# Turning the first two x1 chunks into token columns by DMA transposes of 16-bit planes

## The chip, the cores and the metric

The kernel runs on one core of a Trainium2 chip. The core has TensorE (matrix products, PE in the profile; its weight loads are PEld), VectorE (DVE), ScalarE (ACT), GpSimd (POOL) and SyncE (SP, which here only issues DMAs). Each engine works through its own queue in the order in which the program was written, and semaphores make one engine wait for another. The metric is device microseconds of one execution; lower is better.

## The reference

One encoder layer on x of 512 tokens by 2048 columns, all in float32:

```
h = RMSNorm(x);  q, k, v of A and B = h @ W_in
A = grouped-query attention, axial rotary;  B = dilated windowed attention, partial rotary
x1 = x + concat(RMSNorm(A), RMSNorm(B)) @ W_out
out = RMSNorm(x1 + SwiGLU(RMSNorm(x1)))
```

The change lies between the third line and the fourth. W_out makes x1 with tokens on the partitions (four tiles of 128 tokens), in four chunks of 512 columns. The gate and up products of SwiGLU need x1 the other way round: its columns on the partitions and the 512 tokens along the row, as the operand that TensorE holds. So each 128 x 128 block of x1 has to be transposed, 64 blocks in all.

## The kernel before, in words

**Products.** A float32 operand is split into a high part rounded to the format that TensorE takes fast (ScalarE, a Copy) and the low rest (VectorE, a subtraction). `mm3` (L226) makes three products: high by high (L228), high by low (L229), low by high (L230). The low part of a weight is thus needed at the second matmul. In the gate/up and down products a scheme of seven products of sums (forms) takes the place of eight.

**Units.** The program is a list of units, written out by the loop at L1552 to L1571. In W_out a unit is 128 rows of weights by 512 columns: four token tiles by three matmuls, 12 in all. Mixer A's four chunks come first, then mixer B's four chunks of eight units each, and then the gate/up blocks. Ahead of the matmuls of unit n, `prepare(n)` (L1515) writes: loads of weights up to LOAD_AHEAD = 24.0 planned us ahead at UNIT_US = 2.6 a unit, which is nine units (`Raw.load`, L273, on SP, two units per load); the high part of a weight up to SPLIT_AHEAD = 10.0 ahead, which is unit n+3 (L301, ScalarE); and the low part one unit behind that, unit n+2 (L306, VectorE).

**Side tasks.** Small work is kept in a list `side`. After each unit `give(1.0)` (L725) hands out tasks worth 1.0; a task costs 1.0 unless `weighed` (L674) gives it another cost. So the place of a task in the queues is behind the matmuls of one unit and ahead of `prepare` of the next.

**Around the change.** When mixer B's chunk c is summed up, `post` (L1120) adds it into x1 on VectorE (L1125, four rows), squares it on ScalarE (L1077), and puts tasks into `side`: two empty ones for c = 0 and one for the other chunks (`wait`, L1131), then for each of the chunk's two pairs of column blocks three tasks `h_side(i, half)` (L1165), and at the end `park_x1` (L1152), four DMAs on SP that store x1 in DRAM, where later stages add to it. The last chunk has an order of its own. In `h_side`, halves 0 and 1 transpose four blocks each on TensorE into a PSUM bank (L1171), and ScalarE moves them out with the gain as scale into the tile `pair` (L1174). After half 1 `pair_sums` makes four sums of pieces on VectorE (L379, in `form_sums`). Part 2 splits the pair into high and low parts in the tile `arena`: two casts on ScalarE (L1182), two subtractions on VectorE (L1184).

**A part that the change repeats.** The gate/up blocks already transpose their results by DMA: `planes` (L1255) copies the 32-bit words of a tile into a plane of their 16-bit halves, `turn` (L1258) transposes it by one DMA from SP, and `merge` (L1264) puts the halves together again, all copies on ScalarE.

Of the kernel before, what the change touches and what calls it, by code (L numbers as in the profile page):

```python
# [11 lines left out]
F32 = mybir.dt.float32  # L12
BF16 = mybir.dt.bfloat16
F32R = mybir.dt.float32r
U16 = mybir.dt.uint16
AF = mybir.ActivationFunctionType
# [4 lines left out]
P = 128  # L21
# [3 lines left out]
NT = S // P  # L25
# [41 lines left out]
COLUMN_BLOCKS = 3  # L67
SUM_LEAD = 6
ATTEND_PAST = 4


def f32(ap):
# [4 lines left out]
def encoder_block(ctx, tc, x, w_in, g_q_a, g_k_a, w_out, w_gate_up, w_down, g_final, x_t, gains, c_ident, c_mask,  # L77
                  c_axial, c_partial, out):
    nc = tc.nc
# [3 lines left out]
    sp = ctx.enter_context(tc.tile_pool(name="slots"))  # L83
# [5 lines left out]
    def nm(base):  # L89
        counter[0] += 1  # L90
        return f"{base}_{counter[0]}"

    def slot(base, dtype=F32, shape=(P, 512)):
        return sp.tile(list(shape), dtype, tag="s", name=nm(base))
# [57 lines left out]
    ident, gm, gf, go = fixed[:, :P], fixed[:, P:P + 16], fixed[:, P + 16:P + 32], fixed[:, P + 32:P + 48]  # L152
# [85 lines left out]
    class Pair:  # L238
        def __init__(self):
            self.parts = [sp.tile([P, 512], F32R, tag="tw", bufs=2 * TWINS, name=nm("tw")) for _ in range(2)]  # L240
# [72 lines left out]
    side = deque()  # L313
# [5 lines left out]
    def wait(n):  # L319
        side.extend([lambda: None] * n)  # L320
# [56 lines left out]
    def form_sums(a_l, a_r, b_l, b_r, s1, s2, s3, s4):  # L377
        def tt(out, x, y, op=OP.subtract):
            nc.vector.tensor_tensor(out, x, y, op=op)  # L379
        tt(s1, a_r, b_r, OP.add)  # L380
        tt(s3, a_l, a_r)
        tt(s2, s1, a_l)
        tt(s4, b_l, s2)
# [148 lines left out]
    def rope_partial(q):  # L532
        rot = q.rearrange("p t (h d) -> p t h d", h=4)[:, :, :, :PARTIAL]
        tmp = turning.rearrange("p (t h c) -> p t h c", t=NT, h=4)
        hp = PARTIAL // 2
        for s in range(2):
            nc.vector.tensor_tensor(
                tmp[:, :, :, s * hp:(s + 1) * hp], rot[:, :, :, (1 - s) * hp:(2 - s) * hp],
                ropeb[:, 1, :, s * hp:(s + 1) * hp][:, :, None, :].to_broadcast([P, NT, 4, hp]), op=OP.mult)
        nc.vector.tensor_tensor(rot, rot, ropeb[:, 0][:, :, None, :].to_broadcast([P, NT, 4, PARTIAL]), op=OP.mult)  # L540
        nc.vector.tensor_tensor(rot, rot, tmp, op=OP.add)

    oT = {}
    o_dram = {(g, h): dp.tile([P, 512], F32, tag=f"o{g}{h}", name=f"o{g}{h}")
# [129 lines left out]
    def weighed(cost, f):  # L674
        f.cost = cost
        return f
# [167 lines left out]
    class Half(Unit):  # L844
# [27 lines left out]
        def part(self, j):  # L872
            lo = self.i % 2 * 512
            return (self.duo.hi, self.duo.lo)[j][:, lo:lo + 512]
# [197 lines left out]
    x1 = {}  # L1072
# [6 lines left out]
    def out_chunk(kind, c):  # L1079
        box = {}  # L1080
        base = 0 if kind == "A" else NHA
        order = [6, 7, 0, 1, 2, 3, 4, 5] if (kind, c) == ("B", NC - 1) else list(range(NHA))

        def early(k):
            if (kind, k) not in oS and k >= SPILLED[kind]:
                drain_until(lambda: (kind, k) in oT)
                oS[kind, k] = split(oT.pop((kind, k)), "oS", go[:, base + k:base + k + 1],
                                    at=O_HOMES[kind][2 * k:2 * k + 2] if kind == "A" or k < 7 else None)

        class Back:  # L1090
            def __init__(self, k):
                self.k = k

            def load(self):
                drain_until(lambda: (kind, self.k) in oT)
                self.t = slot("oback")
                nc.sync.dma_start(self.t, o_dram[kind, self.k])

            def split_hi(self):
                hi, lo = oS[kind, self.k] = [place(*h) for h in O_HOMES[kind][2 * self.k:2 * self.k + 2]]  # L1100
                nc.scalar.activation(hi, self.t, AF.Copy, scale=go[:, base + self.k:base + self.k + 1])

            def split_lo(self):
                hi, lo = oS[kind, self.k]
                nc.vector.scalar_tensor_tensor(lo, self.t, go[:, base + self.k:base + self.k + 1], f32(hi),
                                               op0=OP.mult, op1=OP.subtract)

        def mm(u, n):
            k = order[n]
            if n == 0:  # L1110
                box["ps"] = [bank() for _ in range(NT)]
                if kind == "A":
                    whole = slot("x1", F32, (P, NT, 512))
                    x1[c] = [whole[:, t] for t in range(NT)]
                    for t in range(NT):
                        nc.sync.dma_start(x1[c][t], x[0, t * P:(t + 1) * P, c * 512:(c + 1) * 512])
            by_rows(u, n, NHA, lambda i, w, t: mm3(box["ps"][t], cols(oS[kind, order[i]], t * P), w, i == 0,
                                                   i == NHA - 1), post, kind == "A")

        def post(rows):  # L1120
            drain_until(lambda: kind in ro)
            if (kind, c) == ("B", 0) and 0 in rows:
                nc.scalar.activation(slot("table")[:, :1], ones, AF.Silu)
            for t in rows:
                nc.vector.scalar_tensor_tensor(x1[c][t], box["ps"][t], ro[kind][:, t:t + 1], x1[c][t],  # L1125
                                               op0=OP.mult, op1=OP.add)
                release(box["ps"][t])
                if kind == "B" and c < NC - 1:
                    square_x1(c, t)
            if kind == "B" and NT - 1 in rows:  # L1130
                wait(2 if c == 0 else 1)  # L1131
                if c == NC - 1:
                    side.extend(lambda p=p: h_side(2 * c, p, True) for p in range(4))
                    side.append(lambda: [square_x1(c, t) for t in (0, 1)])
                    side.extend(lambda p=p: h_side(2 * c + 1, p, True) for p in range(2))
                    side.append(lambda: park_x1(c))
                    side.append(lambda: [square_x1(c, t) for t in (2, 3)])
                    side.extend(lambda p=p: h_side(2 * c + 1, p, True) for p in range(2, 4))
                    side.append(make_r2)
                    return  # L1140
                for i in (2 * c, 2 * c + 1):
                    for part in range(3):
                        side.append(lambda i=i, part=part: h_side(i, part))
                side.append(weighed(0.0, lambda: park_x1(c)))
        add_chunk(w_out, [(base + k) * P for k in order], [(c * 512, 0, 512)], mm, None,
                  early if kind == "B" or c == 0 else None,
                  (lambda k: [Back(k)] if k < SPILLED[kind] else []) if c == 0 else None, tag="wa" if kind == "A" else "wo")
# [4 lines left out]
    def park_x1(c):  # L1152
        for t in range(NT):
            nc.sync.dma_start(x1_dram[c, t], x1[c][t])

    def pair_sums(w):
        def part(n):
            return w[:, n * 256:(n + 1) * 256]
        a_r, a_l, s3, s2, b_l, b_r, s1, s4 = (part(n) for n in range(8))
        form_sums(a_l, a_r, b_l, b_r, s1, s2, s3, s4)  # L1160

    hf = [False] * (KD // 2)
    hpart = {}

    def h_side(i, half, apart=False):  # L1165
        if half < 2:
            k = 2 * i + half
            c, j = divmod(k, 4)
            ps = bank()
            for n, t in enumerate((2, 3, 0, 1) if half == 0 else range(NT)):  # L1170
                nc.tensor.transpose(ps[:, n * P:(n + 1) * P], x1[c][t][:, j * P:(j + 1) * P], ident)  # L1171
            if half == 0 and not hpart:
                hpart[0] = sp.tile([P, 4 * 512], F32, tag="pair", bufs=1, name=nm("pair"))
            nc.scalar.activation(hpart[0][:, half * 1024:half * 1024 + 512], ps, AF.Copy, scale=gf[:, k:k + 1])  # L1174
            release(ps)
        if half == 1:
            pair_sums(hpart[0])
        if half >= 2:
            src = hpart[0][:, 256:].rearrange("p (f c) -> p f c", c=256)
            for t, part in ((arena[0], src[:, :EARLY]), (arena[1], src[:, EARLY:])):  # L1180
                if half == 2:
                    nc.scalar.activation(t[:, :, i, 0], part, AF.Copy)  # L1182
                if half == 3 or not apart:
                    nc.vector.tensor_tensor(t[:, :, i, 1], part, f32(t[:, :, i, 0]), op=OP.subtract)  # L1184
        if half == (3 if apart else 2):
            hf[i] = True
# [294 lines left out]
    at = [0.0]  # L1481
# [61 lines left out]
    pair = in_turn(twins, TWINS, [P, 2, 512], F32R, "tw")  # L1543
# [85 lines left out]
```

## Time and profile before

| | us |
|---|---|
| median of 3 runs | 1952.29 |
| lowest and highest run | 1951.33, 1952.58 |
| the profiled execution | 1951.23 |
| its span, first to last instruction | 1949.4 |
| granted TensorE clock (1 is full) | 0.999 |
| first and last transpose of x1 on TensorE (L1171) start | 613.8, 691.9 |

A row of the timeline reads: start, duration, engine, line, operation, tile written <- tiles read, shapes, count; in brackets the idle time before it and who ended it. A row of a group gives the least, median and greatest duration in ns and the first and last start. A row of waits gives the waiting engine and line, whom it waited for, the sum in us, how many times, and the longest. For a DMA the timeline has the time that its issue holds the queue; its landing is counted from the start of the issue. All times are microseconds from the start of the span unless marked ns.

### The profile page before, as it was taken

To read this page: it belongs to the slowest core of one execution; us is meant where nothing else is said; L and a number is where in the kernel's file an instruction comes from. 1 tells how busy PE (TensorE), PEld (TensorE's weight loads), DVE (VectorE), ACT (ScalarE), POOL (GpSimd) and SP (SyncE) were. 2 spreads that over 40 slices of the span, in tenths; PEclk is the share of its full clock that TensorE was granted. 3 is DMA by queue.
4 is the path that set the end of the run, shared out by engine and by line. 5 is a ranking of instruction groups with operands and counts; after the bars stand their busy time and mean duration, and the time that the engine had idled before them with its cause. 6 is when DMAs were issued, how large, how long until landed. Compare 5 with 4: busy or idle time off the path is not lost.

```text
span 1949.4 us, 24583 instructions
## 1 busy us (share of the span) xinstructions
PE 1937.3 (99%) x8743; PEld 1599.7 (82%) x8743; DVE 1536.5 (79%) x2012; ACT 1123.3 (58%) x1643; POOL 140.1 (7%) x184
## 2 busy tenths in 40 slices
PE   9999999999999999999999999999999999999998
PEld 7888888888888888888888888888888888888886
DVE  7987768888775697778778777787788978787887
ACT  7755554565455565555555555565555666565555
POOL 1000011000000000000000000000000121111121
PEclk9999999999999999999999999999999999999999
DMA  9677693144342557758767768678587799868865
GB/s 347 233 263 231 212 284 111 59 152 146 103 147 97 184 182 218 268 149 283 233 185 273 224 204 286 183 243 292 141 285 268 212 242 272 229 162 245 235 144 172
DMA packets 252028, 409.30 MB, mean 210 GB/s; under 512 B 58688, under 2 KB 85824, under 8 KB 251776
## 3 DMA queue, kind: packets, MB, share of 16 engines
q1 hardware_dynamic: 221072, 321.12, 50.6%
q0 software_dynamic: 22480, 60.57, 12.4%
q10 hardware_dynamic: 8352, 26.05, 4.1%
q8 instruction: 68, 1.11, 0.2%
q14 instruction: 56, 0.46, 0.1%
HBM read 334.52 MB, written 62.65 MB: 204 GB/s over the span
## 4 chain that ended last, share of the span: by engine, by line
PE 96%; DVE 3%; issue 1%; ACT 0%; DMA 0%; DVEq 0%; POOLq 0%; POOL 0%; SPq 0%; ACTq 0%
PE b L228 31%; PE b L230 31%; PE b L229 31%; PE b L613 1%; PE b L1171 0%; PE b L563 0%; DVE x L1125 0%; DVE w L306 0%; DVE ra L460 0%; DVE tw L896 0%; DVE qA L463 0%; PE b L790 0%; DMA stage<-in_w_in_dram 0%; PE b L574 0%; DVE qA L469 0%
## 5 line engine op out<-in xcount | busy, mean ns | idle before, releaser
L837 ACT ACTIVATE wide<-raw 128x1024 fp32r<-128x1024 f32 x462 | 487.1, 1058 | 455.3 <-PE b L230 265.4
L228 PE MATMUL b<-wide,arena 128*128 128x512 f32 x1848 | 719.6, 389 | 0.0
L840 DVE TENSOR_TENSOR wide<-raw,wide 128x1024 fp32r<-128x1024 f32 x462 | 561.7, 1221 | 200.4 <-ACT wide L837 192.8
L229 PE MATMUL b<-wide,arena 128*128 128x512 f32 x1848 | 719.0, 389 | 0.0
L230 PE MATMUL b<-wide,arena 128*128 128x512 f32 x1848 | 719.0, 389 | 0.0
L229 PEld LDWEIGHTS b<-wide,arena 128*128 128x128 f32 x1848 | 347.0, 188 | 72.1 <-DVE wide L840 0.3
L230 PEld LDWEIGHTS b<-wide,arena 128*128 128x128 f32 x1848 | 347.0, 188 | 71.9
L228 PEld LDWEIGHTS b<-wide,arena 128*128 128x128 f32 x1848 | 347.0, 188 | 71.6
L973 DVE TENSOR_TENSOR raw<-raw,raw 128x1024 f32<-128x1024 f32 x264 | 320.8, 1217 | 10.1 <-DMA raw<-in_w_gate_up_dram 10.1
L229 PE MATMUL b<-tw,arena 128*128 128x512 f32 x396 | 154.3, 390 | 0.6 <-DVE tw L896 0.6
L230 PE MATMUL b<-tw,arena 128*128 128x512 f32 x396 | 154.3, 390 | 0.0
L228 PE MATMUL b<-tw,arena 128*128 128x512 f32 x396 | 154.1, 389 | 0.0
L893 ACT ACTIVATE tw<-stage 128x512 fp32r<-128x512 f32 x140 | 85.4, 628 | 69.4 <-DVE stage L973 43.9
L896 DVE TENSOR_TENSOR tw<-stage,tw 128x512 fp32r<-128x512 f32 x140 | 93.5, 685 | 22.0 <-ACT tw L893 21.9
L228 PE MATMUL b<-w,arena 128*128 128x512 f32 x240 | 95.8, 399 | 0.0
L219 ACT ACTIVATE pTh<-b 128x512 fp32r<-128x512 f32 x64 | 38.2, 597 | 99.8 <-PE b L613 98.1
L230 PE MATMUL b<-w,arena 128*128 128x512 f32 x240 | 93.9, 391 | 0.0
L229 PE MATMUL b<-w,arena 128*128 128x512 f32 x240 | 93.5, 390 | 0.0
L229 PEld LDWEIGHTS b<-tw,arena 128*128 128x128 f32 x396 | 74.3, 188 | 16.7 <-DVE tw L896 1.4
L230 PEld LDWEIGHTS b<-tw,arena 128*128 128x128 f32 x396 | 74.3, 188 | 16.0 <-DVE arena L347 0.3
L228 PEld LDWEIGHTS b<-tw,arena 128*128 128x128 f32 x396 | 74.3, 188 | 15.4
L379 DVE TENSOR_TENSOR pair<-pair 128x256 f32<-128x256 f32 x120 | 46.4, 421 | 46.8 <-ACT pair L1174 23.2
(234 smaller groups left out, 2096.1 us busy)
## 6 DMA issues: line engine op xcount, KB each, us to landing
raw<-in_w_gate_up_dram SPq DMA_DIRECT2D x308, 512.0 KB, 6.3
raw<-in_w_down_dram SPq DMA_DIRECT2D x88, 512.0 KB, 7.7
stage<-in_w_in_dram SPq DMA_DIRECT2D x111, 256.0 KB, 5.3
forms<-pair POOLq DMA_DIRECT2D x22, 896.0 KB, 6.5
fr<-forms ACTq DMA_DIRECT2D x35, 512.0 KB, 6.2
raw<-in_w_out_dram SPq DMA_DIRECT2D x32, 512.0 KB, 4.1
x1d<-s POOLq DMA_DIRECT2D x54, 256.0 KB, 6.8
stage<-in_w_in_dram SPq DMA_DIRECT2D x90, 128.0 KB, 3.5
```

Source lines behind the costliest of these rows:

```text
L219: nc.scalar.activation(hi, src, AF.Copy)
L228: nc.tensor.matmul(dst, ah, bh, start=start, stop=False, skip_group_check=chained)
L229: nc.tensor.matmul(dst, ah, bl, start=False, stop=False, skip_group_check=chained)
L230: nc.tensor.matmul(dst, al, bh, start=False, stop=stop, skip_group_check=chained)
L379: nc.vector.tensor_tensor(out, x, y, op=op)
L613: nc.tensor.transpose(ps[:, t * P:(t + 1) * P], self.p[t][:, kb * P:(kb + 1) * P], ident)
L837: nc.scalar.activation(self.hi, self.src, AF.Copy)
L840: nc.vector.tensor_tensor(self.lo, self.src, f32(self.hi), op=OP.subtract)
L893: nc.scalar.activation(self.pair[:, 0], self.src, AF.Copy)
L896: nc.vector.tensor_tensor(self.pair[:, 1], self.src, f32(self.pair[:, 0]), op=OP.subtract)
L973: nc.vector.tensor_tensor(t[dst], t[src[0]], t[src[1]], op=OP.add if form == "m6" else OP.subtract)
```

## The change

For chunks 0 and 1 of x1 the transposes go by DMA. A class `Turned` holds the steps: `part(t)` copies token tile t (128 x 512 words) into a plane of 1024 16-bit halves on ScalarE, `turn(t)` transposes that plane by one DMA from SP into `words`, and `merge(h)` puts the halves of one column block together on ScalarE. `turned_x1(c)` gives the list of tasks that takes the place of the six `h_side` tasks and the parking at the end: pieces 0 and 1; transposes 0 and 1 with pieces 2 and 3; transposes 2 and 3, then parking; halves 0 and 1; the first pair's split and half 2; half 3 and the second pair's split. Tasks joined by a comma cost 0.5 each. A half is now a merge (two copies for an even one, one for an odd one) and the scaling by the gain. One empty task stands ahead of chunk 0's, not two. Chunks 2 and 3 are transposed on TensorE as before.

```diff
+X1_BY_DMA = 2
+    class Turned:
+        def __init__(self, whole):
+            self.whole, self.planes, self.words = whole, {}, None
+
+        def part(self, t):
+            p = self.planes[t] = slot("plane", U16, (P, 1024))
+            src = self.whole()[:, t].bitcast(U16).rearrange("p (h c s) -> p h s c", h=4, s=2)
+            nc.scalar.activation(p.rearrange("p (h s c) -> p h s c", h=4, s=2), src, AF.Copy)
+
+        def turn(self, t):
+            if self.words is None:
+                self.words = slot("words", U16, (P, NT, 8, P))
+            nc.sync.dma_start_transpose(self.words[:, t], self.planes.pop(t))
+
+        def merge(self, h, runs=((0, NT),)):
+            m, at = slot("merged"), 0
+            for lo, hi in runs:
+                src = self.words[:, lo:hi, 2 * h:2 * h + 2].rearrange("p t s c -> p t c s")
+                dst = m[:, at:at + (hi - lo) * P].bitcast(U16)
+                nc.scalar.activation(dst.rearrange("p (t c s) -> p t c s", c=P, s=2), src, AF.Copy)
+                at += (hi - lo) * P
+            return m
...
+                    x1["whole", c] = whole
...
-                wait(2 if c == 0 else 1)
+                wait(2 if c == 0 and not X1_BY_DMA else 1)
...
+                if c < X1_BY_DMA:
+                    side.extend(turned_x1(c))
+                    return
...
+    def turned_x1(c):
+        turned, i = Turned(lambda: x1["whole", c]), 2 * c
...
+        def half(j):
+            k = 4 * c + j
+            if not hpart:
+                hpart[0] = sp.tile([P, 4 * 512], F32, tag="pair", bufs=1, name=nm("pair"))
+            m = turned.merge(j, ((0, NT),) if j % 2 else ((2, NT), (0, 2)))
+            at = j % 2 * 1024
+            nc.scalar.activation(hpart[0][:, at:at + 512], m, AF.Copy, scale=gf[:, k:k + 1])
+            if j % 2:
+                pair_sums(hpart[0])
+        return [lambda: parts(0, 1), lambda: [turns(0, 1), parts(2, 3)],
+                weighed(0.5, lambda: turns(2, 3)), weighed(0.5, lambda: park_x1(c)), weighed(0.5, lambda: half(0)), weighed(0.5, lambda: half(1)),
+                weighed(0.5, lambda: h_side(i, 2)), weighed(0.5, lambda: half(2)), weighed(0.5, lambda: half(3)),
+                weighed(0.5, lambda: h_side(i + 1, 2))]
```

More of the change, by code (lines that the diff above doesn't have):

```diff
@@ L1160, in pair_sums, with parts, turns @@
         form_sums(a_l, a_r, b_l, b_r, s1, s2, s3, s4)
+    def turned_x1(c):
+        turned, i = Turned(lambda: x1["whole", c]), 2 * c
+        def parts(*rows):
+            for t in rows:
+                turned.part(t)
+        def turns(*rows):
+            for t in rows:
+                turned.turn(t)
+        def half(j):
[11 more added lines that the diff above has]
+                weighed(0.5, lambda: h_side(i + 1, 2))]
     hf = [False] * (KD // 2)
```

## The prediction

> **What bounds the kernel now.** I read the page first (shares and chain), then the waits of TensorE, the stages by windows, and the timeline of each engine between 600 and 700 us, where the changed work lies.
>
> ```profile
> span 1949.4 us, 24583 instructions
> PE 1937.3 (99%) x8743; PEld 1599.7 (82%) x8743; DVE 1536.5 (79%) x2012; ACT 1123.3 (58%) x1643; POOL 140.1 (7%) x184
> PE 96%; DVE 3%; issue 1%; ACT 0%; DMA 0%; DVEq 0%; POOLq 0%; POOL 0%; SPq 0%; ACTq 0%
> ```
> TensorE is busy for 99% of the span and carries 96% of the chain: any time taken from it comes off the end, and any wait put into it is added. From 600 to 760 us its only wait is this one:
>
> ```profile
> PE b L1171 <- DVE x L1125: 0.5, 2, 0.3
> ...
> 612.00:631.00 19.00, 19.00 (x93) 15.71 (x92) 11.22 (x20) 12.13 (x21) 0.00 (x0) 1.00 0.42 139
> 631.00:650.00 19.00, 18.81 (x91) 15.32 (x90) 12.00 (x20) 10.61 (x21) 0.00 (x0) 1.00 0.69 230
> ```
> In the two windows (PE, PEld, DVE, ACT, POOL, granted clock, DMA share, GB/s) ScalarE works 12.1 and 10.6 of 19 us. That spare third is what the change wants to use.
>
> **What is removed.** I number the 24 units of mixer B's chunks 1, 2 and 3 from 1 to 24; unit 0 is the last of chunk 0, whose end releases the first changed chunk.
>
> ```profile
> L1171 PE MATMUL b<-fixed,x x64: 270/272/331, 613.8 to 691.9; 128*128 128x128 f32 x64
> 604.69 0.39 PE L228 MATMUL b<-w,oSh 128*128 128x512 f32 x1
> ...
> 607.41 0.95 PE L399 MATMUL b<-fixed,acc 128*128 128x1 f32 x8
> 608.22 0.49 PE L228 MATMUL b<-w,arena 128*128 128x512 f32 x1
> ...
> 613.81 0.60 PE L1171 MATMUL b<-fixed,x 128*128 128x128 f32 x4
> ...
> 617.02 0.60 PE L1171 MATMUL b<-fixed,x 128*128 128x128 f32 x4
> 632.06 0.39 PE L228 MATMUL b<-w,arena 128*128 128x512 f32 x1
> 656.19 0.39 PE L228 MATMUL b<-w,arena 128*128 128x512 f32 x1
> ```
> A unit of 12 matmuls without transposes takes 607.41 - 604.69 = 2.72 us (0.227 per matmul: the 0.39 overlaps the next). A unit with one group of four transposes takes 617.02 - 613.81 = 3.21, so a group costs 0.49, not the 4 x 0.272 that its rows seem to say. Units 3 to 8 hold four groups: 632.06 - 613.81 - 6 x 2.72 = 1.93. Two chunks: TensorE loses 2 x 1.93 = **3.9 us of work**. Eight evictions on ScalarE (L1174) go too, but eight scalings of the same shape replace them.
>
> **What is added on ScalarE.** The same three operations exist in the gate/up blocks, at the same shapes:
>
> ```profile
> L1255 ACT ACTIVATE pair<-s x40: 1038/1041/1045, 762.6 to 1453.4; 128x1024 uint16<-128x1024 uint16 x40
> 762.57 1.99 ACT L1255 ACTIVATE pair<-s 128x1024 uint16<-128x1024 uint16 x2
> L1264 ACT ACTIVATE pair<-turned x60: 672/682/1184, 789.7 to 1481.7; 128x512 uint16<-128x512 uint16 x40, 128x1024 uint16<-128x1024 uint16 x20
> ```
> Two planes back to back take 1.99, so the second adds 0.95; with the same 0.08 to 0.09 of overlap a merge of 512 adds 0.60 and one of 1024 adds 1.08 (1.17 for one alone, between the 0.68 and the 1.184 of its row). Per chunk: 4 x 0.95 + 4 x 0.60 + 2 x 1.08 = 8.4 us. What ScalarE does already per chunk follows from these:
>
> ```profile
> 610.71 0.63 ACT L1077 ACTIVATE j<-x 128x512 f32<-128x512 f32 x1 [6.49 <-DVE x L1125]
> 613.31 1.14 ACT L301 ACTIVATE w<-raw 128x512 fp32r<-128x512 f32 x2
> 614.51 0.69 ACT L1174 ACTIVATE pair<-b,fixed 128x512 f32<-128x512 f32 x1
> 619.23 0.63 ACT L1182 ACTIVATE arena<-pair 128x512 fp32r<-128x512 f32 x1 [0.37 <-DVE pair L379]
> 620.03 1.28 ACT L1182 ACTIVATE arena<-pair 128x1280 fp32r<-128x1280 f32 x1 [0.16 <-DVE pair L379]
> ```
> Squares 613.31 - 610.71 = 2.6, eight weight splits at 1.14 / 2 = 0.57, four scalings at 0.61, two times two casts at 0.55 + 1.20: 13.1. With the 8.4 it is **21.5 us of work in a chunk of 8 x 2.72 = 21.8**. ScalarE is full before it has waited once, and each queue runs in the order written: behind a waiting merge stand the weight splits, and TensorE waits for those.
>
> **The wait for the transposes.**
>
> ```profile
> L1258 SPq DMA_TRANSPOSE turned<-pair x40: 1231/1534/3287, 763.6 to 1455.6; - x40
> DMA to landing us min/median/max: 3.1/4.8/7.6
> 839.79 1.26 SPq L1258 DMA_TRANSPOSE turned<-pair  x1
> ...
> 843.72 4.98 SPq L1258 DMA_TRANSPOSE turned<-pair  x2
> ```
> One transposes a 128 x 1024 plane, eight blocks. The queue is held 1.23 us at least, and (4.98 / 2) 2.5 each for two in a row there, where weight loads lie between them; landing is 3.1 to 7.6 after the start of the issue. Here four follow each other with no load between, on quiet DMA engines. I take 1.4 per issue and 3.3 to land, near the least of both rows.
> [...]
>
> **The sum, on the clock of before.** VectorE's steps:
>
> ```profile
> 609.92 2.73 DVE L1125 SCALAR_TENSOR_TENSOR x<-b,fixed,x 128x512 f32<-128x512 f32 x4 [1.16 <-POOL fixed L210]
> 618.38 1.56 DVE L379 TENSOR_TENSOR pair<-pair 128x256 f32<-128x256 f32 x4 [3.12 <-ACT pair L1174]
> 619.85 0.69 DVE L306 TENSOR_TENSOR w<-raw,w 128x512 fp32r<-128x512 f32 x1
> 621.34 1.49 DVE L1184 TENSOR_TENSOR arena<-pair,arena 128x1280 fp32r<-128x1280 f32 x1 [0.20 <-ACT arena L1182]
> ```
> The order written (with one idle unit in place of two ahead of chunk 0's tasks): the split of unit n+3 precedes unit n; the low part (L306) follows one unit later. So pieces 0 and 1 come behind the split of unit 4, pieces 2 and 3 behind that of unit 5, halves 0 and 1 behind that of unit 7, and ahead of the low part of unit 7. Halves 2 and 3 with all sums and casts stand ahead of the low part of unit 9.
> ScalarE: split 4 at 613.3, planes 0 and 1 done at 614.9 and 615.9, split 5, planes 2 and 3 at 617.4 and 618.35, splits 6 and 7 until 619.4. SP: issues at 614.9, 616.3, 617.7, 619.1; the fourth lands at **622.4**. ScalarE stands 3.0 us.
> Half 0 is 0.60 + 0.60 + 0.61, half 1 is 1.08 + 0.69: done at 626.0. Four pair sums (1.56) and the low part of unit 7 (0.68): 628.3. TensorE, 0.23 into unit 7, wants it at 613.81 + 4 x 2.72 + 0.23 = 624.9: a stall of 3.4.
> ScalarE goes on: split 8, cast after the first sum, wide cast after the fourth at 627.6, to 628.9; half 2 to 630.6; split 9; half 3 done at 633.0; pair sums 634.6; wide cast 635.9; its low part on VectorE (1.49) 637.4; the low part of unit 9 at **638.1**. TensorE would want it at 630.4, and got to this point at 632.3 before: **5.8 us later than before** after one chunk, the 1.93 already taken off.
> VectorE then does the low part of unit 10 and starts the x updates of chunk 1 at 638.7, 28.8 after the 609.92 of chunk 0. The same steps follow: the low part of unit 17 at 638.1 + 28.8 = 666.9, against 656.19 + 0.23 = 656.4 before: **10.5 later**. Chunk 2, still on TensorE, has its x updates done at 670.2; its first transposes could start at 669.4, a wait of 0.8 that this chunk did not have (the two waits of before are in chunks 1 and 3). Sum: **+11.3 us**, 1951.23 + 11.3 = 1962.5 for the profiled execution (which lies 1.06 under the median), **1963.6** for the median.
> Bounds: with issues at 1.25 and landing at 3.1 the fourth lands at 621.75, 0.65 sooner in each chunk: +10.0. If the transposes took no time at all, ScalarE would be free 3.0 sooner in each: +5.3. Landing at 7.6 adds 4.3 to each: +19.9. The new tiles need SBUF slots (a plane 2 KB a partition, the words 8 KB); I take no wait for them, since x1 leaves its own 8 KB sooner than before; one that did come would shift this chain one for one.
>
> **What costs nothing.** Everything on SP behind the transposes:
>
> ```profile
> 598.65 0.37 SPq L273 DMA_DIRECT2D raw<-in_w_out_dram  x1
> 604.29 0.37 SPq L273 DMA_DIRECT2D raw<-in_w_out_dram  x1
> L1154 SPq DMA_DIRECT2D x1d<-x x16: 320/443/1648, 615.1 to 694.0; - x16
> raw<-in_w_out_dram SPq DMA_DIRECT2D x32, 512.0 KB, 4.1
> 668.00:687.00 19.00, 18.67 (x90) 15.11 (x89) 13.26 (x21) 10.65 (x14) 0.00 (x0) 1.00 0.04 15
> ```
> The load of units 11 and 12 (598.65) stands ahead of the transposes; that of 13 and 14, issued at 604.29 before, now waits for four transposes and four parks (about 4 x 0.5) until some 622.6 and lands by 626.7, while its split is due after 640. The gate/up loads have more room: the DMA engines stood at 0.04 from 668 to 687. Without that cover a late weight would cost its lateness in full. Parking sooner is on nobody's way.
>
> **The rivals.**
> *A, faster: ScalarE keeps ahead.* All 3.9 us come off: 1948.4. For it: the spare third in the windows, and that ScalarE no longer waits for transposes on TensorE. Against: 21.5 of 21.8. It decides at the low part of unit 9: ready before 632.3 instead of 638.1. Transposes that cost nothing give 3.0 of these 5.8; the other 2.8 would have to come from 15.7 us of steps with rows. At about that point stands *B, no change*: 1952.3.
> *C, the transposes land late,* 7.6 as in the slowest row: 1952.3 + 19.9 = 1972.2. Against it: loads lay between those.
> *D, TensorE runs at half pace after the stalls.* Its idle times here would be 3.4 before unit 7, 4.3 before unit 9, 2.7 and 4.3 in the next chunk; nothing of the kind is in this trace, whose clock stays at 1.00.
>
> ```profile
> 1.26 3.17 PE L186 MATMUL b<-warm 128*128 128x512 bf16 x7 [1.26 <-DVE warm L181]
> ```
> The first seven matmuls of the kernel took 0.45 each, twice the 0.227. If a unit behind each stall ran so, it would take 2.7 more; behind all but the last stall the next one swallows it, so 1963.6 + 2.7 = 1966.3. [...]
>
> **How the numbers follow.** The forecast, the ScalarE chain, 0.63 (its steps have rows; the landing is the loose term). D 0.12, C 0.10, A 0.10, B 0.05. The range leaves out A, B and the top of C: from 1957 (transposes free) to 1973 (C). Slower by over 0.2%, 3.9 us, about what can be told from no change: 0.63 + 0.12 + 0.10 = 0.85; within it 0.05; faster 0.10.
>
> **What would show it.** TensorE's waits list L229 behind w of L306, four times, 2.5 to 4.5 us, in units 7, 9, 15 and 17; ScalarE waits for the words by DMA about 3 us per chunk and is else busy without a gap; L1171 has 32 instructions. Wrong would be: no wait of TensorE on L306 between 610 and 670 us, or splits that stand ahead of the merges on ScalarE.

## The result and the profile after

| | before | after |
|---|---|---|
| median, us | 1952.43 (4 runs, 1951.33 to 1953.03) | 1967.12 (4 runs, 1966.90 to 1967.82) |
| profiled execution, us | 1951.23 | 1966.90 |
| its span, us | 1949.4 | 1965.1 |

The change makes the kernel slower: ratio 1.0078, 95% interval 1.0066 to 1.0090, or 14.7 us. The forecast was 11.3 more, 1963.6, with a range of 1957 to 1973.

Line numbers have moved: L228 to L230 are now L229 to L231, L306 is L307, L1125 is L1150, L1171 is L1224, L1154 is L1182. New are L551 (plane), L556 (transpose), L563 (merge) and L1207 (scaling by the gain). The two executions also stand 1.31 us apart at the end of unit 0 (L399 at 607.41 before, L400 at 608.72 after); where times of both are compared, that is taken off.

First the page, then the waits of TensorE from 600 to 780 us, then the same stretch by windows (PE, PEld, DVE, ACT, POOL, granted clock, DMA share, GB/s).

```profile
span 1965.1 us, 24569 instructions
PE 1940.9 (99%) x8711; PEld 1601.4 (81%) x8711; DVE 1537.4 (78%) x2012; ACT 1141.4 (58%) x1663; POOL 140.5 (7%) x184
...
PE b L230 <- DVE w L307: 12.1, 4, 5.1
PE b L1224 <- DVE x L1150: 0.3, 1, 0.3
...
612.00:631.00 19.00, 14.38 (x64) 11.58 (x62) 6.29 (x12) 13.54 (x24) 0.00 (x0) 0.97 0.70 187
631.00:650.00 19.00, 16.53 (x61) 13.15 (x62) 12.61 (x19) 15.50 (x25) 0.00 (x0) 0.85 0.20 53
650.00:668.00 18.00, 15.57 (x61) 12.11 (x59) 7.64 (x14) 13.36 (x19) 0.00 (x0) 0.91 0.98 300
668.00:687.00 19.00, 16.41 (x71) 13.43 (x72) 12.04 (x18) 10.72 (x21) 0.00 (x0) 0.91 0.65 224
```
The page's shares hardly move, and TensorE is "99%" in both. The stage shows it: four waits of TensorE for the low part of a weight, 12.1 us where there were none. TensorE's busy time falls from 19.00 to 14.38 of 19 us in the first window, with 64 matmuls begun in place of 93. The granted clock, 1.00 before, is 0.85 to 0.97.

The four waits on TensorE's timeline, and the pace behind them:

```profile
625.99 0.39 PE L229 MATMUL b<-w,arena 128*128 128x512 f32 x1
631.53 0.80 PE L230 MATMUL b<-w,arena 128*128 128x512 f32 x1 [5.14 <-DVE w L307]
632.12 0.63 PE L231 MATMUL b<-w,arena 128*128 128x512 f32 x1
632.55 0.63 PE L229 MATMUL b<-w,arena 128*128 128x512 f32 x1
...
636.75 0.40 PE L230 MATMUL b<-w,oSh 128*128 128x512 f32 x1
...
641.63 0.50 PE L230 MATMUL b<-w,arena 128*128 128x512 f32 x1 [1.95 <-DVE w L307]
...
660.48 0.75 PE L230 MATMUL b<-w,arena 128*128 128x512 f32 x1 [2.24 <-DVE w L307]
...
664.24 0.40 PE L230 MATMUL b<-w,arena 128*128 128x512 f32 x1
...
670.59 0.63 PE L230 MATMUL b<-w,arena 128*128 128x512 f32 x1 [2.77 <-DVE w L307]
...
674.34 0.39 PE L230 MATMUL b<-w,arena 128*128 128x512 f32 x1
...
674.80 0.60 PE L1224 MATMUL b<-fixed,x 128*128 128x128 f32 x4
```
Each is the second matmul of a unit (7, 9, 15, 17), the first that needs the weight's low part. Behind three of them matmuls follow each other at 0.43 us (632.12 to 632.55) in place of 0.227, until the rows that close each stretch.

TensorE's account: from the end of unit 0 to the first transpose of chunk 2 it took 658.91 - 607.41 = 51.5 us before and 674.80 - 608.72 = 66.1 after, 14.6 more. The waits are 12.1, and 0.16 more each (the last matmul's 0.39 overlaps by that much in a stream): 12.8. The slow stretches took, beyond the 0.227 a matmul, 2.5 (12 matmuls from 631.53 to 636.75), 1.7 (9 from 660.48), 1.7 (9 from 670.59), and 0.1 behind unit 9: 6.0. Taken off: 3.9 of transposes and a wait of 0.3 that chunk 1's transposes had. 12.8 + 6.0 - 4.2 = 14.6.

Where the low parts were: ScalarE's timeline (planes, first merges, and the first square of chunk 1), the issues and landings of the transposes, and VectorE's timeline.

```profile
615.14 1.99 ACT L551 ACTIVATE plane<-x 128x1024 uint16<-128x1024 uint16 x2
...
625.45 1.27 ACT L563 ACTIVATE merged<-words 128x512 uint16<-128x512 uint16 x2 [4.85 <-DMA words<-plane]
...
642.87 0.63 ACT L1101 ACTIVATE j<-x 128x512 f32<-128x512 f32 x1 [2.39 <-DVE x L1150]
...
654.38 1.28 ACT L563 ACTIVATE merged<-words 128x512 uint16<-128x512 uint16 x2 [2.93 <-DMA words<-plane]
```
```profile
616.21 5.48 SPq L556 DMA_TRANSPOSE words<-plane  x4
647.07 5.38 SPq L556 DMA_TRANSPOSE words<-plane  x4
DMA to landing us min/median/max: 3.2/3.3/5.0
```
```profile
611.23 2.73 DVE L1150 SCALAR_TENSOR_TENSOR x<-b,fixed,x 128x512 f32<-128x512 f32 x4 [1.16 <-POOL fixed L211]
630.79 0.68 DVE L307 TENSOR_TENSOR w<-raw,w 128x512 fp32r<-128x512 f32 x1
640.89 1.29 DVE L307 TENSOR_TENSOR w<-raw,w 128x512 fp32r<-128x512 f32 x2
642.09 2.72 DVE L1150 SCALAR_TENSOR_TENSOR x<-b,fixed,x 128x512 f32<-128x512 f32 x4
671.05 2.72 DVE L1150 SCALAR_TENSOR_TENSOR x<-b,fixed,x 128x512 f32<-128x512 f32 x4
```
ScalarE stands 4.85 us at chunk 0's first merge and 2.93 at chunk 1's. The low parts of units 7 (630.79) and 9 (640.89) stand behind what those merges feed. The x updates (L1150) show the length of one round: 642.09 - 611.23 = 30.9 us for the first, 671.05 - 642.09 = 29.0 for the second, where TensorE has only 21.8 us of matmuls. ScalarE is not busy throughout a round: besides the wait for the words it stands 2.39 us until VectorE has updated x, and some 1.6 us until VectorE has made the pair sums.

### The profile page after: what moved, and what is told of

Read it like the earlier page. It is cut to its first block, busy times and chain, and to the rows that moved or that the text cites. A ratio compares the mean times of both kernels' runs of the same rounds, so it can differ in the third digit from the quotient of the medians.

```text
span 1965.1 us, 24569 instructions
## 1 busy us (share of the span) xinstructions
PE 1940.9 (99%) x8711; PEld 1601.4 (81%) x8711; DVE 1537.4 (78%) x2012; ACT 1141.4 (58%) x1663; POOL 140.5 (7%) x184
## 4 chain that ended last, share of the span: by engine, by line
PE 93%; DVE 3%; ACT 2%; issue 1%; DMA 1%; SPq 0%; POOL 0%; DVEq 0%; POOLq 0%; ACTq 0%
PE b L230 30%; PE b L231 30%; PE b L229 30%; PE b L637 1%; DVE pair L380 0%; ACT plane L551 0%; PE b L587 0%; ACT arena L1235 0%; DVE w L307 0%; ACT merged L563 0%; ACT w L302 0%; PE b L814 0%; DMA raw<-in_w_out_dram 0%; ACT j L1101 0%; DVE ra L461 0%
## 5 line engine op out<-in xcount | busy, mean ns | idle before, releaser
L229 PE MATMUL b<-wide,arena 128*128 128x512 f32 x1848 | 719.6, 389 | 0.0
L231 PE MATMUL b<-wide,arena 128*128 128x512 f32 x1848 | 719.0, 389 | 0.0
L230 PE MATMUL b<-wide,arena 128*128 128x512 f32 x1848 | 718.9, 389 | 0.0
L229 PEld LDWEIGHTS b<-wide,arena 128*128 128x128 f32 x1848 | 346.9, 188 | 72.0
L230 PEld LDWEIGHTS b<-wide,arena 128*128 128x128 f32 x1848 | 346.9, 188 | 71.8
L231 PEld LDWEIGHTS b<-wide,arena 128*128 128x128 f32 x1848 | 346.8, 188 | 71.9
L230 PE MATMUL b<-tw,arena 128*128 128x512 f32 x396 | 154.3, 390 | 0.6 <-DVE tw L920 0.6
L229 PE MATMUL b<-tw,arena 128*128 128x512 f32 x396 | 154.1, 389 | 0.0
L231 PE MATMUL b<-tw,arena 128*128 128x512 f32 x396 | 154.1, 389 | 0.0
L230 PE MATMUL b<-w,arena 128*128 128x512 f32 x240 | 96.3, 401 | 12.1 <-DVE w L307 12.1
L229 PE MATMUL b<-w,arena 128*128 128x512 f32 x240 | 96.8, 403 | 0.0
L231 PE MATMUL b<-w,arena 128*128 128x512 f32 x240 | 96.1, 401 | 0.0
L230 PEld LDWEIGHTS b<-tw,arena 128*128 128x128 f32 x396 | 74.3, 188 | 16.6 <-DVE tw L920 1.4
L229 PEld LDWEIGHTS b<-tw,arena 128*128 128x128 f32 x396 | 74.3, 188 | 15.6
L231 PEld LDWEIGHTS b<-tw,arena 128*128 128x128 f32 x396 | 74.4, 188 | 15.4
```

Of the source, the lines that this page charges most:

```text
L229: nc.tensor.matmul(dst, ah, bh, start=start, stop=False, skip_group_check=chained)
L230: nc.tensor.matmul(dst, ah, bl, start=False, stop=False, skip_group_check=chained)
L231: nc.tensor.matmul(dst, al, bh, start=False, stop=stop, skip_group_check=chained)
```

## The experiments

**The theory, Q:** one chunk's steps, in the order written, form a chain through ScalarE and VectorE that is longer than the 21.8 us of matmuls beside it, and the weight splits queue behind it. **Rivals:** *T*, only the wait for the transfers counts; *M*, only the merges' work; *P*, the parking and loads next to the transposes; *H*, TensorE's half pace behind its stalls; *L*, the splits are merely written too close to their use. All times below are medians, against the median of before on the same chip, which lay between 1951.95 and 1952.75. The waits are those of the one execution that was profiled. In the runs' kernels some lines lie elsewhere: the transposes of x on TensorE at L1224 to L1229, the x updates at L1150 to L1152.

**One chunk.** `X1_BY_DMA = 2` becomes 1.

> Only chunk 0 goes by DMA. Queue order (weight splits stand behind the merges on ScalarE and VectorE): the two waits of units 7 and 9 stay as they are, those of units 15 and 17 are gone, so 8 to 9 us over the kernel before, 1961. If the loss were shared evenly by the two chunks: half of 14.7, 1959.8. If it came from the second chunk alone: no slower than before.

1959.42 against 1952.55, ratio 1.0037 (1.0024 to 1.0050). The waits of TensorE:

```profile
PE b L230 <- DVE w L307: 6.9, 2, 5.2
```
The waits of units 7 and 9 stay and those of 15 and 17 go, as Q has it. But the time is 6.9 us more, about half of 14.7, as in an even split (1959.8), and not the 8 to 9 that Q was expected to give. Each chunk costs about the same.

**No transfer.** The merges read the planes untransposed, so the forms of chunks 0 and 1 are made from unturned data:

```diff
-            p = self.planes[t] = slot("plane", U16, (P, 1024))
+            if self.words is None:
+                self.words = slot("words", U16, (P, NT, 8, P))
+            p = self.words[:, t].rearrange("p a c -> p (a c)")
...
-            nc.sync.dma_start_transpose(self.words[:, t], self.planes.pop(t))
+            pass
```

> The eight DMA transposes are left out and the merges read the untransposed planes, so the output is wrong in the forms of chunks 0 and 1; every operation of ScalarE and VectorE stays. Queue order on a full ScalarE: unit 7 waits 0.5, unit 9 about 4.4, unit 17 about 2, net 5 to 6 us over before, 1958. If the wait for the transposes alone is the cause: 3.9 us under before, 1948.5.

1958.74 against 1952.55, ratio 1.0030 (1.0018 to 1.0042): 6.2 slower, where the bound with free transposes was 5.3.

```profile
PE b L230 <- DVE w L307: 6.7, 3, 4.2
```
With no transfer at all TensorE still waits 6.7 us for low parts, and the x updates of chunk 1 start 635.99 - 610.06 = 25.9 us after those of chunk 0, still more than 21.8. T falls as the whole cause: without the transfers 14.7 - 6.2 = 8.5 us of the loss are gone and 6.2 stay.

**No merges.** The 12 merges are left out; the scaling reads the high halves as numbers, so the forms of chunks 0 and 1 hold other values:

```diff
-            m = turned.merge(j, ((0, NT),) if j % 2 else ((2, NT), (0, 2)))
+            m = turned.words[:, :, 2 * j + 1]
...
-            nc.scalar.activation(hpart[0][:, at:at + 512], m, AF.Copy, scale=gf[:, k:k + 1])
+            nc.scalar.activation(hpart[0][:, at:at + 512].rearrange("p (t c) -> p t c", t=NT), m, AF.Copy, scale=1e-5)
```

> The 12 merges are left out: the scaling reads the transposed high halves as numbers, so the forms of chunks 0 and 1 are wrong; planes, transposes and their wait stay. A chunk's chain is then 4.6 us shorter after landing. Chain of ScalarE work plus landing: about 4.4 us over before, 1957. If the landing is the cause by itself: 1967 as before this edit.

1955.32 against 1952.75, ratio 1.0016 (1.0007 to 1.0026): 2.6 slower.

```profile
PE b L230 <- DVE w L307: 5.1, 3, 2.4
```
Without the merges, 12.1 of the 14.7 us are gone, though the transfers are all there. With the 8.5 of the run before that is more than 14.7, so the two don't add up: each takes up slack that the other then lacks. M alone falls as well: the time is still 2.6 above before, although TensorE has 3.9 us less to do, and waits for low parts stay. (The profiled execution took 1958.55, 3.2 above the median, and chunk 0's fourth plane was late in it, so most runs will have waited less than its 5.1 us.)

**Parking last.** `park_x1` goes behind the last task of its chunk.

```diff
-                weighed(0.5, lambda: turns(2, 3)), weighed(0.5, lambda: park_x1(c)), weighed(0.5, lambda: half(0)), weighed(0.5, lambda: half(1)),
+                lambda: turns(2, 3), weighed(0.5, lambda: half(0)), weighed(0.5, lambda: half(1)),
...
-                weighed(0.5, lambda: h_side(i + 1, 2))]
+                weighed(0.5, lambda: h_side(i + 1, 2)), weighed(0.0, lambda: park_x1(c))]
```

> Parking goes back behind the last task of the chunk, so that no store follows the transposes on SP. If the stores made the fourth transpose of chunk 0 land 1.7 us late: unit 7 waits 3.5 in place of 5.2, and 1.7 us come off, 1965.4. If parking has nothing to do with it: 1967 as it was.

1966.52, ratio 1.0071 (1.0056 to 1.0086): 0.6 below the change's 1967.12, with overlapping intervals.

```profile
624.00 1.27 ACT L563 ACTIVATE merged<-words 128x512 uint16<-128x512 uint16 x2 [4.81 <-DMA words<-plane]
```
ScalarE waits as long for chunk 0's fourth plane as with parking right behind it.

**A quiet queue.** With parking last, weight loads follow the transposes at once. Here SyncE waits for the fourth plane before any other DMA:

```diff
...
+            if rows[-1] == 3:
+                mark = sp.tile([P, 1], F32, tag="mark", bufs=1, name=nm("mark"))
+                nc.gpsimd.tensor_copy(mark, turned.words[:, 3, 0, :2].bitcast(F32))
+                nc.sync.dma_start(mark_dram[c], mark)
```

> Behind each chunk's fourth transpose SyncE first stores one column that GpSimd has copied out of the fourth plane's words, so that no DMA starts before the fourth plane has landed; parking and weight loads come after it. In the changed kernel the fourth transpose of chunk 0 landed 5.0 us after its issue and the other seven 3.2 to 3.5. Theory 1, the parking or weight loads that start right behind it take its share of the DMA engines: it lands 3.2 to 3.5 us after the issue here, unit 7 waits 3.4 to 3.8 us instead of 5.1 and the end comes up to 1.7 us sooner, 1965.4. Theory 2, four transposes in a row hold each other up whatever follows: the landing stays at 4.8 to 5.0 us, unit 7 waits 5.1 and the time stays at 1967. If the held loads were what a later unit waits for, a wait on a weight load would stand in TensorE's list between 640 and 660 us; I expect none, since their splits are due after 640.

1966.87 against 1951.95, ratio 1.0074 (1.0060 to 1.0088): no gain. GpSimd's timeline for both chunks, ScalarE's for chunk 0, and a row of the DMA queues from 623.0 to 624.3 us, where chunk 0's transposes end (queue, kind, packets, MB, share of 16 engines):

```profile
625.12 0.18 POOL L1203 COPY mark<-words 128x1 f32<-128x1 f32 x1 [13.92 <-DMA words<-plane]
654.26 0.18 POOL L1203 COPY mark<-words 128x1 f32<-128x1 f32 x1 [28.96 <-DMA words<-plane]
...
625.17 1.28 ACT L563 ACTIVATE merged<-words 128x512 uint16<-128x512 uint16 x2 [4.57 <-DMA words<-plane]
...
q8 instruction: 1, 0.02, 4.8%
```
P falls: no parking and no weight load runs, and the fourth plane of chunk 0 is still late (4.7 us). That four transposes in a row hold each other up doesn't fit either: chunk 1's four, just as close, all landed after 3.2 to 3.4. One thing did run: an instruction fetch (the profile's kind "instruction"), a single packet of 16 KB on queue q8, from 623.05 to 624.04 (4.8% of 16 engines over 1.3 us is 1.0 us of one engine). All but two of the plane's packets were through by 623.1. The last two, of 4 bytes each, came at 624.02, just as the fetch ended, and the two waiting engines start at 625.1. Behind chunk 1's fourth plane there was no fetch; its last packet came at 653.6, and GpSimd started 0.6 us later.

**Splits further ahead.** The chunks 1 to 3 of W_out get their high parts five units ahead, not three.

```diff
+            if tag == "wo" and pieces[0][0] > 0:
+                units[-1].ahead = 15.5
```

> The changed kernel with the weight splits of mixer B's chunks 1 to 3 written five units ahead in place of three. If only the place of the splits behind the merges is wrong, two more units (5.4 us) of lead remove all waits but a rest: 1952 or less. If the chain of a chunk (28 us and more on ScalarE and VectorE, against 21.8 us on TensorE) is too long wherever the splits stand, the waits for weights shrink but x1 of the third chunk comes late, some 8 to 11 us of waits of the transposes for x: 1965.

1965.39, ratio 1.0063 (1.0050 to 1.0077).

```profile
PE b L230 <- DVE w L307: 8.2, 3, 3.2
PE b L1226 <- DVE x L1152: 3.8, 3, 3.2
```
L falls. This lead only moves the waits: 12.1 us for low parts become 8.2, and 3.8 us for x appear, at the transposes of the later chunks (8 to 11 were expected there). The x updates of chunk 1 start 641.31 - 612.19 = 29.1 us after those of chunk 0, as long as in the change. That no other lead would do better is argued from this and was not run.

**Fillers.** Extra matmuls of an unused product (21, 17, 10, 17) ahead of units 7, 9, 15 and 17 keep TensorE busy while it would wait.

```diff
...
+                    fills.update({share["now"] + 7: (21, 10)[c], share["now"] + 9: 17})
...
+        for _ in range(fills.get(n, 0)):
+            nc.tensor.matmul(banks[0], oS["B", 0][0][:, :P], units[n - 1].w[0], start=True, stop=True)
```

> The changed kernel with 21, 17, 10 and 17 matmuls on old operands ahead of units 7, 9, 15 and 17, into an unused bank, so that TensorE works where it waited. If the half pace behind the waits (0.427 us a matmul) comes from TensorE's idle time, the pace stays 0.227 and the 1.7 us lost behind unit 17 come off, less 0.7 of a wait for x that then shows: about 1966. If it comes from something else, the pace falls as before and the time stays at 1967 or rises.

1966.92, ratio 1.0072 (1.0058 to 1.0086), as the change itself.

```profile
PE b L230 <- DVE w L307: 2.5, 4, 1.3
...
631.00:650.00 19.00, 18.64 (x82) 14.87 (x81) 11.82 (x18) 15.50 (x26) 0.00 (x0) 1.00 0.25 58
654.45 1.27 ACT L563 ACTIVATE merged<-words 128x512 uint16<-128x512 uint16 x2 [4.29 <-DMA words<-plane]
```
The granted clock is 1.00 (0.85 in this window of the change) with waits of 1.33 us at most (1.95 to 5.14 in the change), so it is the idle time that brings the half pace. The total doesn't move: H is no cause of the 14.7 as a whole. What it costs net stays unsettled here, since chunk 1's fourth plane was also late in this run (a wait of 4.29, not 2.93): 1.4 us, where 1.0 was expected back from the pace.

**Spread.** The same work in both chunks, but each step is placed behind a fixed later unit, when its data should be there: planes after 1 and 2 units, halves and pair splits of chunk 0 after 7, 10, 12, 13, 13 and 14, with four empty tasks ahead of chunk 2's transposes.

```diff
...
-                    side.extend(turned_x1(c))
+                    for late, f in turned_x1(c):
+                        hook(share["now"] + late, f)
...
+        lates = (1, 2, 3, 7, 10, 12, 13, 13, 14) if c == 0 else (1, 2, 3, 7, 9, 10, 10, 11, 12)
```

> The same operations, but each task is written behind a later unit: halves and splits of chunk 0 behind units 7 to 14, of chunk 1 behind units 15 to 20, chunk 2's tasks three units later than before. Queue order: no wait of TensorE for a weight's low part, the 3.9 us of removed transposes come off, 1948 to 1949. If it is the volume of work added on ScalarE and VectorE, wherever it stands: no better than 1960.

1951.20 against 1952.55, ratio 0.9995 (0.9986 to 1.0005): some 16 us below the change with the same work, but no clear change from before, where 1948 to 1949 was expected.

```profile
PE b L229 <- ACT arena L1238: 1.4, 1, 1.4
PE b L230 <- DVE wide L864: 0.9, 1, 0.9
PE b L1227 <- DVE x L1150: 0.3, 1, 0.3
```
No wait for a low part of W_out is left; TensorE is busy for all of the 56 us from 612 to 668. From 633 to 655 us ScalarE works 20.9 of 22 us here and TensorE is busy throughout: a nearly full ScalarE costs nothing by itself. That is Q: not the work but its place in the queues cost 14.7 us. What is left of the 3.9 gained is paid where the gate/up products open (1.4 and 0.9), since chunks 2 and 3 now come later.

**Four ways to keep the rest.** *Packed* is Spread with two of chunk 2's and 3's transposes per unit and one empty task ahead of chunk 3's. *Spread and ahead* is Spread up to two units earlier with splits four units ahead (12.0). *One chunk spread* is the first experiment with `lates = (1, 2, 3, 6, 6, 7, 7, 10, 11)`. *Spread on GpSimd* gives the planes to the engine that stood idle in this stage, and puts the halves earlier:

```diff
-            nc.scalar.activation(p.rearrange("p (h s c) -> p h s c", h=4, s=2), src, AF.Copy)
+            nc.gpsimd.tensor_copy(p.rearrange("p (h s c) -> p h s c", h=4, s=2), src)
...
+        lates = (1, 2, 3, 7, 9, 11, 11, 12, 13) if c == 0 else (1, 2, 3, 6, 6, 9, 10, 10, 11)
```

> As the spread kernel, but two transposes of chunk 2 go behind one unit, so that chunk 3's tasks start where they did before. The spread kernel came out 1.35 us under before, with 2.6 us of new waits where the gate/up blocks open. If those came from chunk 3's delayed tasks alone, they go, and the whole 3.9 us are left: 1948.6 to 1949.2. If the removed transposes are worth less than 3.9 us: 1951.

1955.34 against 1952.75, ratio 1.0012 (1.0003 to 1.0021).

```profile
684.77 0.30 PE L1227 MATMUL b<-fixed,x 128*128 128x128 f32 x1 [3.76 <-DVE x L1150]
```

> The spread kernel with chunk 2's tasks one unit earlier, no empty unit ahead of chunk 3's, and the weight splits of mixer B's chunks 1 to 3 four units ahead in place of three. If late work of chunks 2 and 3 at the opening of the gate/up blocks was all that kept the spread kernel from the 3.9 us, the waits of 2.6 us there go: 1948.5 to 1949.5. If ScalarE and VectorE are too full up to that opening, waits come back at chunk 3's x or in the first gate/up units: 1951 to 1954.

1954.96 against 1952.64, ratio 1.0012 (1.0003 to 1.0021).

```profile
PE b L230 <- DVE w L307: 2.9, 3, 1.6
PE b L1229 <- DVE x L1152: 1.7, 2, 1.5
```

> Only chunk 0 by DMA, its halves behind units 6, 7, 10 and 11 and the splits behind 7 and 11, chunk 1's and 2's tasks three and two units later than before, chunk 3's where they were. Half of the removed work, 1.9 us, with room on ScalarE: 1950.5. If moving chunks 1 and 2 back costs as much: 1952.5 or more.

1952.31 against 1952.64, ratio 1.0000 (0.9991 to 1.0008).

```profile
PE b L1227 <- DVE x L1150: 1.8, 2, 1.5
```

> The spread kernel with the planes copied by GpSimd, which is idle there, so that ScalarE has 7.6 us less to do; chunk 2's tasks one unit earlier, no empty unit ahead of chunk 3's. If ScalarE's fullness is what is left and a plane takes GpSimd under 2.5 us: no waits, 1948.5 to 1949.5. If a plane takes it 3.5 or more, or it slows VectorE: 1951 or more.

1950.43 against 1952.64, ratio 0.9990 (0.9981 to 0.9999).

```profile
PE b L1227 <- DVE x L1150: 1.7, 2, 1.5
...
L551 POOL COPY plane<-x x8: 1033/1040/1500, 611.2 to 632.9; 128x1024 uint16<-128x1024 uint16 x8
```
All four were expected lower than they came. *Packed* and *Spread and ahead* are slower than Spread: pulling chunk 2 forward meets x of chunk 3 before VectorE has it (3.76 us), and earlier steps meet the splits again (2.9). In *One chunk spread* the waits for chunk 3's x (1.8) are as much as the 1.9 removed. *Spread on GpSimd* is the best version, 2.2 us below before with an interval that only just excludes no change; as the best of five orders tried, it may owe part of that to chance. Its eight planes cost 1.04 us each on GpSimd, what the row of such a copy on ScalarE says (1.041), and leave ScalarE free for the splits. Of the 3.9 us removed, 1.7 goes into two waits for chunk 3's x.

## Why the prediction was nearly right

- **Sign and mechanism: right.** It named four waits of TensorE for low parts in units 7, 9, 15 and 17, from a ScalarE that is full (21.5 of 21.8 us) before it waits. The profile has these four and 32 instructions on the transposing line. Taking the transfers away left +6.2 where the sum had +5.3; placing the same steps elsewhere took all the waits for these low parts away. Of its two reasons, that ScalarE is full and that the splits stand behind a waiting merge, the second is the one shown: in Spread ScalarE is nearly as full, without harm.
- **The sizes of the four waits: wrong, mostly.** The sum has 3.4, 4.3, 2.7 and 4.3 us; they were 5.14, 1.95, 2.24 and 2.77, and only the last lies in the 2.5 to 4.5 that was named as a sign. The first grew with the late landing. The second and the fourth shrank because TensorE, at half pace behind units 7 and 15, came 2.5 and 1.7 later to units 9 and 17.
- **"Else busy without a gap": wrong.** ScalarE stands some 4 us a round for VectorE besides the wait for the words. The sum itself has these steps of VectorE in its chain, so its length came out right.
- **Removed, 3.9 us: right.** TensorE's account closes with it to within 0.1.
- **Issues and landing, 1.4 and 3.3: right but for one.** Four issues take 5.4 to 5.5, 1.37 each, and the median landing is 3.3. The fourth plane of chunk 0 took 5.0. The step "the fourth lands at 622.4" is the term that was mis-sized. On the clock of before the first issue began at 616.21 - 1.31 = 614.9, as forecast, and the fourth at 614.9 + 3 x 1.37 = 619.0, but it landed at 625.4 - 1.31 = 624.1: the 1.7 is all in this landing. Unit 7 then waited 5.14 in place of 3.4, and the first round took 30.9 in place of 28.8, +2.1. (The 2.5 per issue that the prediction read off the row at 843.72 has no load between its two issues; loads stand before and behind them.)
- **The second round: right.** Chunk 1's fourth plane came in 3.3, and the round took 29.0 where 28.8 was forecast, +0.2.
- **The wait of 0.8 for chunk 2's x: swallowed.** Half pace behind unit 17 made TensorE 1.7 later, so x was there in time: +0.9 net. This is rival D's mechanism with D's rule (only the last stall counts), 1.7 where D had 2.7, held as a rival at 0.12. So 11.3 + 2.1 + 0.2 + 0.9 = 14.5, of the 14.6 in TensorE's account and the 14.7 in the medians. D's 1966.3 lies nearer to the measured 1967.12 than the forecast's 1963.6, but in part by luck: D brought 0.9 net where it had 2.7, and the late landing, which D didn't have, brought 2.1.
- **Rivals A and B** fell on the chain that they had against them: ScalarE didn't keep ahead. **C** fell: the landing was 5.0 at most, not 7.6.
- **What costs nothing: held.** No weight load appears among TensorE's waits, though loads stood behind transposes and parks; with SyncE held longer still (the quiet queue) none appeared. ScalarE waited for none either, nor for a slot of the new tiles. (VectorE's list names a weight load for 8.5 us ahead of the pair sums at 629.32; but those read only the pair, which ScalarE finished at 629.28.)

**Open.** Why the fourth plane of a group lands late. The runs have 22 such planes. Ten landed 4.5 to 5.0 us after their issue: chunk 0's in nine of the twelve kernels that transpose by DMA, the change among them, and chunk 1's in Fillers. In each of these ten cases an instruction fetch (a 16 KB packet on queue q8) began 1.9 to 3.0 us after the issue. Twelve landed in time, after 3.1 to 3.3; beside ten of them no fetch was under way. But with splits further ahead and in Spread and ahead a fetch began 2.6 and 2.7 us after the issue of chunk 0's plane, which landed in time all the same. So the fetch may be the cause, but no run moved it or left it out, and it is not shown. Nor was the net cost of the half pace isolated.

## What to carry to other kernels

Spare time of an engine is no free room if its queue holds what the bounding engine waits for: add up the work per round and lay it out in queue order, with every wait in it, before moving anything there. A step that waits for a DMA belongs behind the point where its data is there, or on an engine that nobody waits for; here the same instructions cost 14.7 us in one order and nothing in another. When the bounding engine stalls, read the granted clock behind the stall too.

## What the runs showed of the hardware that was not expected

- **Behind some stalls TensorE ran at half clock, for 3.41 or 6.83 us, behind others it didn't.** In the change the granted clock is at half from 629.85 for 6.83 us, from 660.57 for 3.41 and from 670.81 for 3.41, behind the waits of units 7, 15 and 17; behind that of unit 9 it is 1.00. Two neighbouring stretches of 3.41 us each of the change, of Splits further ahead and of Spread on GpSimd (PE busy and, before the last two columns, the granted clock):

```profile
657.16:660.57 3.41, 1.17 (x6) 0.65 (x4) 2.27 (x6) 2.84 (x5) 0.00 (x0) 1.00 0.95 307
660.57:663.98 3.41, 3.41 (x8) 2.71 (x9) 2.56 (x3) 3.38 (x6) 0.00 (x0) 0.50 1.04 399
...
628.30:631.71 3.41, 1.76 (x8) 1.13 (x6) 2.58 (x6) 2.70 (x4) 0.00 (x0) 1.00 0.96 303
631.71:635.13 3.42, 2.04 (x9) 1.69 (x10) 2.02 (x3) 3.35 (x6) 0.00 (x0) 1.00 0.44 152
...
676.92:680.33 3.41, 1.68 (x10) 1.01 (x9) 3.41 (x6) 1.26 (x3) 0.00 (x0) 1.00 0.00 0
680.33:683.75 3.42, 3.42 (x12) 2.73 (x11) 2.21 (x2) 1.14 (x3) 0.00 (x0) 0.50 0.02 5
```
  The length of a wait alone didn't decide. In the change the clock was at half behind a wait of 2.24 us (unit 15) and at 1.00 behind one of 1.95 (unit 9). In Splits further ahead matmuls followed each other at 0.23 us behind a wait of 3.04 that ended at 633.10, and at 0.43 from 642.23 to 644.78, behind a wait of 2.01. The wait of 3.04 lies in both of this run's stretches above, with 1.65 and 1.38 us of idle time. In Spread on GpSimd waits of 1.46 and 0.27 lie in one stretch, 1.73 us of idle time together, and half clock follows. With fillers, where no wait was over 1.33, the clock was 1.00 from 612 to 687 us. What decides was not shown.
- **The end of a transposing DMA came 1.4 us late on an otherwise quiet queue.** In the change a plane of eight blocks landed 3.2 to 3.5 us after its issue in 7 of 8 cases, and four in a row started 1.37 us apart; the eighth took 5.0. In the quiet queue, where the median was 3.3, chunk 0's fourth plane took 4.7: its last two packets came at 624.02, 0.9 us behind the rest and just as a 16 KB instruction fetch ended (see Open). In rows of windows such a fetch is easily overlooked, since a packet counts where it starts: from 623.25 to 624.00 us, with the fetch under way, the DMA share there is 0.00.
